# One stream tile for the residual's inputs, and the first mixer's adaLN units at one per product unit

## The chip, the cores and the metric

The kernel runs on one core of a Trainium2 chip. Its time is the device time of one execution in microseconds (us); where several runs were made, the median is given. A profile is one execution taken by the hardware profiler. The engines are named as there: PE (TensorE, matmuls), PEld (its weight loads), DVE (VectorE), ACT (ScalarE), POOL (GpSimd), SP (the engine that only issues transfers here).

## What is computed

A trunk of two layers on x of 256 tokens by 2048 columns, in float32. Each layer has two sub-layers, a token mixer and a SwiGLU feed-forward, and each sub-layer (numbered 0 to 3) is

```python
shift, scale, gate = split(silu(c) @ ada_w + ada_b)          # adaLN, from one row c
y = f(x * (1 + scale) + shift)
x = layer_norm(ALPHA * x + (1 + gate) * y, ln_g, ln_b)
```

Layer 0's mixer has an mLSTM group (8 heads) and an RWKV-7 group (16 heads) on one input projection, and one output projection; layer 1's has retention and gated DeltaNet heads. The feed-forward is `(silu(h @ wg) * (h @ wu)) @ wd` with 5632 hidden columns. All weights, some 650 MB, are read once.

## The kernel before

**Products.** All large products are made of *units*: a tile of 128 x 2048 weights (1 MB) is loaded into one of three `raw` tiles by SP (L690, in `raw`), split into a high and a low part, `hi` by ACT (L713) and `lo` by DVE (L714), and used by 24 matmuls of 128x128x512 (L728 to L730, in `part`). `product` (from L739) strings units together: four for 512 output columns of an input projection, two for half an output projection. It uses two of the three PSUM banks called `g`. After each unit it calls `fill(rate)`, which adds the rate to a credit and starts an adaLN unit for each whole credit, up to `ada_limit`.

**adaLN units.** `ada_unit` (from L635) computes 128 of the 6144 columns of one sub-layer's shift, scale and gate: a load of 1 MB and one multiply-and-sum on DVE over 128 x 2048 (L649). There are 192 units, 48 for each sub-layer. Units 0 to 31 run in the start-up (`first_products`). Where their tile is depends on `homes`: in the first mixer it is one of the same three `raw` tiles that the weights use, taken in program order; in the feed-forward parts it is `za` or `zt` in turn, two tiles of 8 KB per partition with one buffer each; in the second mixer it is `za` or `raw` in turn. The first mixer itself uses `za` for the channels of the RWKV heads (`chan`, L1394) and both mixers use `zt` for pairs of token blocks (`half`, L1134); the first product of a feed-forward part splits one weight tile into `zt`.

**First mixer.** `mixer_ab` (from L1801) runs four batches of RWKV heads. Between them (`after`) it makes eight products of four units, 32 units; it returns the last mLSTM group, `mlstm_group(1, direct)`, as a generator that makes four more products, 16 units, when `mix_out` advances it. With the rate 48.0 / 32 and the limit 80, the units 32 to 79 are all started within the first 32 product units. The gate of sub-layer 0 needs the units below 48, the norm at the end of `mix_out` all 80.

**Output and residual.** `mix_out` (from L1872) runs the output projection in two halves of the inner dimension, four blocks of 512 columns each. After each block of the first half, `first_sum` copies the banks to y (ACT) and `residual` (from L848) does, for each of the two 128-token tiles, y = y * gate (L858), adds ALPHA * (offset row) (L860), multiplies x by the scale row (L861) and adds ALPHA * x (L862). In sub-layer 0 there are no rows (x is the input itself) and only L858 and L862 are left. x comes by `x_block` (L827, 128 x 512) and the rows by `ln_rows` (L844, each broadcast to 128 x 512), each load 256 KB into a tile called `t2`, of which there are three, handed out in program order. After each block of the second half `last_sum` (from L864) multiplies the banks by the gate into a `t2` tile (L870), adds it to y (L871) and takes statistics (L872); L870 is what empties the bank. The feed-forward (`ffn`, from L951) runs its inner dimension in thirds and calls `residual` after the blocks of the second third. The gate row itself goes through DRAM (`gate_rows`, from L674).

**Order.** The program text is only a priority. `Plan` simulates all instructions with a cost for each, the tiles' buffers, and transfers at a fixed rate, and from that writes down for each engine, SP among them, a fixed order in which it then works (`impose`, L522). Tiles of one name are handed out in program order.

Of the kernel before, what the change touches and what calls it, by code (L numbers as in the profile page):

```python
# [16 lines left out]
ALU = mybir.AluOpType  # L17
# [4 lines left out]
P = 128  # L22
T = 256
NT = T // P
# [6 lines left out]
ALPHA = 4.0 ** 0.25  # L31
# [497 lines left out]
class Trunk:  # L529
# [292 lines left out]
        v.tensor_tensor(out, out, z[:], ALU.mult)  # L822


    def x_block(self, xsrc, t, n):
        xb = self.t2([P, 512])
        self.nc.sync.dma_start(xb[:], xsrc[P * t:P * t + P, 512 * n:512 * n + 512])  # L827
        return xb

    def first_sum(self, y, banks, n):  # L830
        for t in range(NT):
            self.nc.scalar.activation(y[t][:, 512 * n:512 * n + 512], banks[t][:], AF.Copy)
# [3 lines left out]
            o = y[t][:, 512 * n:512 * n + 512]  # L836
            self.nc.vector.tensor_tensor(o, banks[t][:], o, ALU.add)

    def ln_rows(self, sub, n):

        out = []
        for j in range(2):
            w = self.t2([P, 512])
            self.nc.sync.dma_start(w[:], self.ins["lnrow"][2 * sub + j:2 * sub + j + 1, 512 * n:512 * n + 512].to_broadcast([P, 512]))  # L844
            out.append(w)
        return out

    def residual(self, y, x, n):  # L848

        v = self.nc.vector  # L850
        xsrc, sub = x
        s = slice(512 * n, 512 * n + 512)
        if sub is not None:
            g, b = self.ln_rows(sub, n)
        for t in range(NT):
            xb = self.x_block(xsrc, t, n)
            o = y[t][:, s]
            v.tensor_tensor(o, o, self.gate[:, s], ALU.mult)  # L858
            if sub is not None:
                v.scalar_tensor_tensor(o, b[:], ALPHA, o, ALU.mult, ALU.add)  # L860
                v.tensor_tensor(xb[:], xb[:], g[:], ALU.mult)  # L861
            v.scalar_tensor_tensor(o, xb[:], ALPHA, o, ALU.mult, ALU.add)  # L862

    def last_sum(self, y, banks, n, stats, ts=range(NT)):  # L864
        v = self.nc.vector
# [1030 lines left out]
def body(tc, ins, out):  # L1896
    with ExitStack() as stack:
        k = Trunk(tc, ins, out, stack)
        k.setup()
        k.ada_limit = 32  # L1900
        h, early = k.first_products()
        x = (ins["x"], None)
        k.ada_limit = 80
        side = k.mixer_ab(h, 48.0 / 32, early)
        x, h = k.mix_out(ins["o_ab"], x, 0, side)
        x, h = k.ffn(0, x, h)
        k.ada_limit = 176
        k.mixer_cd(h, 32.0 / 44)
        x, h = k.mix_out(ins["o_cd"], x, 2)
        k.ffn(1, x, h)  # L1910
        plan = Plan(tc, tc.nc, 250, k.after)
        plan.prepare(0)
        order, _ = plan.run([x.bass_priority for x in plan.ins])
        plan.impose(order)
# [18 lines left out]
```

## Time and profile before

| | us |
|---|---|
| median of 3 runs | 2764.85 |
| lowest, highest | 2756.81, 2773.10 |
| the profiled execution | 2755.91 |
| its span | 2754.2 |
| DVE on adaLN units, the 82 in `raw` tiles | 187.4 |
| RWKV batches and their products | about 120 to 600 |
| output projection of layer 0, with the norm | about 600 to 735 |
| output projection of layer 1, with the norm | about 1895 to 2020 |

In what follows a row of a view by stretch gives the stretch, its length, and for PE, PEld, DVE, ACT and POOL the busy time and (x) the number of instructions, then the granted TensorE clock as a share of full speed, the mean busy share of the 16 DMA engines, and GB/s. A row of a view of waits gives the waiting engine, tile and line, what it waited for, and the time in total, the number of times and the longest. In a timeline a row gives the start, the duration, engine, line, operation, the tile written and those read, the count, and in brackets the idle time before it with what ended it. A row of the DMA issues gives the count, the size and the median time from issue to landing.

### The profile page before, as it was taken

How to read it: one execution, taken by the hardware profiler on the slowest of the kernel's cores; microseconds unless marked ns; L12 is line 12 of the kernel's file. 1: busy time of each engine (PE TensorE's matmuls, PEld its weight loads, DVE VectorE, ACT ScalarE, POOL GpSimd, SP SyncE). 2: the span in 40 equal slices, each digit the busy share in tenths (PEclk: the TensorE clock that was granted, in tenths of full speed). 3: DMA queues.
4: the chain of work that ended last, by engine and by line, in shares of the span. 5: the costliest groups of instructions: out<-in, count | busy, mean ns of one | idle time of the engine just before them, and what ended most of it. 6: DMA issues, size and time to landing. Idle time of an engine off the chain costs nothing.

```text
span 2754.2 us, 33686 instructions
## 1 busy us (share of the span) xinstructions
PE 2627.3 (95%) x12906; PEld 2155.3 (78%) x12906; DVE 2005.0 (73%) x3153; ACT 1272.4 (46%) x1706; POOL 76.8 (3%) x88
## 2 busy tenths in 40 slices
PE   5598999999999999999999999999999999999997
PEld 3476777788788888888888888888778888888886
DVE  7899887658777777767767989875866664557457
ACT  2364545557644444434446654444354444443442
POOL 0000100110000000000000101000000000000000
PEclk9899999999999999999999999999999999999999
DMA  9988775226578888778856776665657675556554
GB/s 394 358 297 300 253 287 207 92 93 211 202 302 303 311 320 315 286 251 309 311 194 227 272 282 220 259 231 204 226 200 274 259 271 188 196 213 240 192 186 165
DMA packets 109819, 681.60 MB, mean 247 GB/s; under 512 B 12437, under 2 KB 15705, under 8 KB 31577
## 3 DMA queue, kind: packets, MB, share of 16 engines
q1 hardware_dynamic: 108506, 677.36, 67.0%
q8 instruction: 101, 1.65, 0.2%
q10 hardware_dynamic: 1152, 2.10, 0.2%
q14 instruction: 60, 0.49, 0.0%
HBM read 668.89 MB, written 10.52 MB: 247 GB/s over the span
## 4 chain that ended last, share of the span: by engine, by line
PE 75%; DVE 6%; issue 3%; DMA 3%; ACT 2%; POOL 0%; DVEq 0%; SPq 0%; ACTq 0%; POOLq 0%
PE g L730 23%; PE g L728 23%; PE g L729 23%; DVE lo L714 1%; PE m L974 1%; ACT hi L713 1%; DMA t<-x 1%; DMA t<-lnrow 1%; DMA za<-ada 1%; DVE raw L649 0%; PE m L1254 0%; PE m L909 0%; PE c L1432 0%; DVE t L870 0%; DMA raw<-w_ab 0%
## 5 line engine op out<-in xcount | busy, mean ns | idle before, releaser
L714 DVE TENSOR_TENSOR lo<-raw,hi 128x1024 fp32r<-128x1024 f32 (+2 forms) x802 | 972.4, 1215 | 594.1 <-ACT hi L713 589.6
L713 ACT ACTIVATE hi<-raw 128x1024 fp32r<-128x1024 f32 (+2 forms) x802 | 842.3, 1053 | 1117.1 <-PE g L730 1028.5
L728 PE MATMUL g<-hi,h 128*128 128x512 f32 (+2 forms) x2312 | 908.8, 394 | 53.7 <-ACT h L792 39.5
L729 PE MATMUL g<-lo,h 128*128 128x512 f32 (+2 forms) x2312 | 907.0, 392 | 4.6 <-DVE lo L714 4.6
L730 PE MATMUL g<-hi,h 128*128 128x512 f32 (+2 forms) x2312 | 905.7, 392 | 0.0
L728 PEld LDWEIGHTS g<-hi,h 128*128 128x128 f32 x2312 | 439.3, 190 | 148.4 <-ACT h L792 42.4
L729 PEld LDWEIGHTS g<-lo,h 128*128 128x128 f32 x2312 | 440.2, 190 | 97.1 <-DVE lo L714 8.8
L730 PEld LDWEIGHTS g<-hi,h 128*128 128x128 f32 x2312 | 439.6, 190 | 86.6 <-issue 2.0
L728 PE MATMUL g<-hi,a 128*128 128x512 f32 x920 | 361.0, 392 | 5.8 <-DVE t L870 5.8
L729 PE MATMUL g<-lo,a 128*128 128x512 f32 x920 | 359.9, 391 | 0.5 <-DVE lo L714 0.5
L730 PE MATMUL g<-hi,a 128*128 128x512 f32 x920 | 359.8, 391 | 0.0
L728 PEld LDWEIGHTS g<-hi,a 128*128 128x128 f32 x920 | 173.4, 189 | 42.1 <-DVE t L870 6.3
L729 PEld LDWEIGHTS g<-lo,a 128*128 128x128 f32 x920 | 173.5, 189 | 36.2 <-DVE lo L714 0.9
L730 PEld LDWEIGHTS g<-hi,a 128*128 128x128 f32 x920 | 173.4, 188 | 35.8
L649 DVE SCALAR_TENSOR_TENSOR raw<-raw,silu_c 128x2048 f32<-128x2048 f32 x82 | 187.4, 2286 | 16.5 <-DMA raw<-ada 8.7
L649 DVE SCALAR_TENSOR_TENSOR za<-za,silu_c 128x2048 f32<-128x2048 f32 x56 | 127.9, 2284 | 3.5 <-DMA za<-ada 3.5
L649 DVE SCALAR_TENSOR_TENSOR zt<-zt,silu_c 128x2048 f32<-128x2048 f32 x38 | 86.8, 2284 | 1.4 <-DMA zt<-ada 1.4
L1438 DVE SCALAR_TENSOR_TENSOR f<-c,cols_sb,f 128x253 f32<-128x253 f32 (+2 forms) x120 | 56.1, 475 | 3.0 <-ACT f L1435 2.4
L1639 POOL TENSOR_SCALAR s<-cons_sb,log_alpha 128x128 f32<-128x128 f32 x16 | 15.9, 1006 | 1008.6 <-DVE log_alpha L1583 867.6
L649 DVE SCALAR_TENSOR_TENSOR a<-a,silu_c 128x2048 f32<-128x2048 f32 x16 | 36.4, 2286 | 0.2
L912 ACT ACTIVATE t<-m,affine 128x128 f32<-128x128 f32 x96 | 34.9, 470 | 0.1
L1254 PE MATMUL m<-y 64*128 64x256 f32 x128 | 30.6, 413 | 3.6 <-DVE a L1257 3.4
(480 smaller groups left out, 2095.7 us busy)
## 6 DMA issues: line engine op xcount, KB each, us to landing
raw<-gu SPq DMA_DIRECT2D x176, 1024.0 KB, 4.7
raw<-dn SPq DMA_DIRECT2D x88, 1024.0 KB, 4.8
raw<-ada SPq DMA_DIRECT2D x82, 1024.0 KB, 5.4
raw<-w_cd SPq DMA_DIRECT2D x60, 1024.0 KB, 4.8
za<-ada SPq DMA_DIRECT2D x56, 1024.0 KB, 7.0
raw<-w_ab SPq DMA_DIRECT2D x48, 1024.0 KB, 5.0
zt<-ada SPq DMA_DIRECT2D x38, 1024.0 KB, 6.9
a<-ada SPq DMA_DIRECT2D x16, 1024.0 KB, 17.0
```

The costliest lines, as they stand in the source:

```text
L649: v.scalar_tensor_tensor(w[:], w[:], 1.0, self.sc[:], ALU.mult, ALU.mult, accum_out=m[:, i:i + 1])
L713: nc.scalar.activation(hi[:, :2 * n], ws, AF.Copy)
L714: nc.vector.tensor_tensor(lo[:, :2 * n], ws, hi[:, :2 * n], ALU.subtract)
L728: mm(o, ah, wh, start=start and k == 0, stop=False)
L729: mm(o, ah, wl, start=False, stop=False)
L730: mm(o, al, wh, start=False, stop=stop and k == 3)
L912: nc.scalar.activation(h32[:, j, :], b[:, P * j:P * j + P], AF.Identity, bias=self.ab[:, sub + 1, 16 + k:17 + k], scale=self.ab[:, sub + 1 ...
L974: nc.tensor.transpose(b[:, P * k:P * k + P], gs[:, t, P * k:P * k + P], self.ident)
L1254: mm(b[:, T * x:T * x + T], bk[r, c, x, t, :], ar[r, c, t].rearrange("p x s -> p (x s)"), start=True, stop=True)
L1438: v.scalar_tensor_tensor(o[:, d:T], b[:, T * j:T * j + T - d], self.col(wname, 4 * (tile0 + i + j) + 3 - d), o[:, d:T], ALU.mult, ALU.add)
L1639: nc.gpsimd.tensor_scalar(L[:], sl, self.gl[:, t, 4 * g + j:4 * g + j + 1], None, ALU.mult)
```

## The change

`residual` no longer loads its blocks one by one. For every pair of blocks (n even) `stream` loads x for both token tiles and 1024 columns into one tile `za` (1 MB), and the two rows for 1024 columns into one tile `zt` (two loads of 512 KB); the arithmetic reads slices of these. And in the first mixer the rate of adaLN units goes from 48 / 32 to 48 / 48 for each product unit.

```diff
-    def x_block(self, xsrc, t, n):
-        xb = self.t2([P, 512])
-        self.nc.sync.dma_start(xb[:], xsrc[P * t:P * t + P, 512 * n:512 * n + 512])
-        return xb
...
-    def ln_rows(self, sub, n):
-
-        out = []
+    def stream(self, x, n):
+
+        xsrc, sub = x
+        s = slice(512 * n, 512 * n + 1024)
+        xs = self.own([P, NT, 1024], "za", 1)
+        self.nc.sync.dma_start(xs[:], xsrc[:, s].rearrange("(t p) c -> p t c", p=P))
+        if sub is None:
+            return xs, None
+        gb = self.own([P, 2, 1024], "zt", 1)
         for j in range(2):
-            w = self.t2([P, 512])
-            self.nc.sync.dma_start(w[:], self.ins["lnrow"][2 * sub + j:2 * sub + j + 1, 512 * n:512 * n + 512].to_broadcast([P, 512]))
-            out.append(w)
-        return out
+            self.nc.sync.dma_start(gb[:, j, :], self.ins["lnrow"][2 * sub + j:2 * sub + j + 1, s].to_broadcast([P, 1024]))
+        return xs, gb
 
     def residual(self, y, x, n):
 
         v = self.nc.vector
-        xsrc, sub = x
-        s = slice(512 * n, 512 * n + 512)
-        if sub is not None:
-            g, b = self.ln_rows(sub, n)
+        if n % 2 == 0:
+            self.rest = self.stream(x, n)
+        xs, gb = self.rest
+        s, c = slice(512 * n, 512 * n + 512), slice(512 * (n % 2), 512 * (n % 2) + 512)
         for t in range(NT):
-            xb = self.x_block(xsrc, t, n)
+            xb = xs[:, t, c]
             o = y[t][:, s]
             v.tensor_tensor(o, o, self.gate[:, s], ALU.mult)
-            if sub is not None:
-                v.scalar_tensor_tensor(o, b[:], ALPHA, o, ALU.mult, ALU.add)
-                v.tensor_tensor(xb[:], xb[:], g[:], ALU.mult)
-            v.scalar_tensor_tensor(o, xb[:], ALPHA, o, ALU.mult, ALU.add)
+            if gb is not None:
+                v.scalar_tensor_tensor(o, gb[:, 1, c], ALPHA, o, ALU.mult, ALU.add)
+                v.tensor_tensor(xb, xb, gb[:, 0, c], ALU.mult)
+            v.scalar_tensor_tensor(o, xb, ALPHA, o, ALU.mult, ALU.add)
...
-        side = k.mixer_ab(h, 48.0 / 32, early)
+        side = k.mixer_ab(h, 48.0 / 48, early)
```

## The prediction

> **What bounds the kernel now.** I read the page first, then what TensorE (PE) waited for, then PE and VectorE (DVE) by stretch around the two places that the edit touches.
>
> ```profile
> span 2754.2 us, 33686 instructions
> PE 2627.3 (95%) x12906; PEld 2155.3 (78%) x12906; DVE 2005.0 (73%) x3153; ACT 1272.4 (46%) x1706; POOL 76.8 (3%) x88
> ```
>
> PE is busy for 2627.3 of 2754.2 us, so all that any edit beside PE can win is the 127 us in which it idles, and time in which it runs at a lower granted clock. Who ends that idle time:
>
> ```profile
> PE g L728 <- ACT h L792: 50.0, 7, 14.4
> ...
> PE g L728 <- DVE t L870: 5.8, 1, 5.8
> ```
>
> The first line, 50 us, is the wait for the first activations at the start, which the edit leaves alone. The second is one single stall of 5.8 us behind `last_sum`; the edit of the residual touches it. Now the first mixer, by stretch. The columns of the first view are PE, PEld, DVE, ACT and POOL busy with their counts, then granted clock, DMA share and GB/s; the second view is the same for the adaLN line L649 alone, where each unit counts twice, its accumulator read being an instruction of its own.
>
> ```profile
> 120.00:205.00 85.00, 78.68 (x371) 61.70 (x372) 75.56 (x129) 50.15 (x89) 3.75 (x2) 0.96 0.84 298
> 205.00:260.00 55.00, 45.18 (x179) 33.81 (x177) 50.36 (x111) 20.46 (x25) 2.10 (x3) 0.94 0.81 301
> 260.00:300.00 40.00, 39.52 (x355) 33.29 (x355) 32.16 (x56) 19.71 (x38) 0.10 (x1) 1.00 0.75 272
> 300.00:371.00 71.00, 65.28 (x277) 48.31 (x274) 65.72 (x159) 32.04 (x56) 7.01 (x5) 0.98 0.78 284
> 371.00:470.00 99.00, 95.14 (x586) 74.64 (x585) 78.25 (x201) 50.57 (x94) 4.38 (x5) 0.97 0.66 232
> 470.00:547.00 77.00, 72.58 (x487) 57.48 (x486) 53.20 (x173) 44.64 (x90) 7.33 (x11) 0.93 0.27 91
> 547.00:650.00 103.00, 101.92 (x686) 86.45 (x685) 65.55 (x164) 64.75 (x110) 13.70 (x19) 1.00 0.37 129
> ```
> ```profile
> 205.00:260.00 55.00, 22.90 (x20) 0.94 0.81 301
> 260.00:300.00 40.00, 13.76 (x12) 1.00 0.75 272
> 300.00:371.00 71.00, 25.23 (x22) 0.98 0.78 284
> 371.00:470.00 99.00, 20.62 (x18) 0.97 0.66 232
> ```
>
> From 205 to 260 us DVE is busy 92% of the time, 22.9 of 50.4 us of it with ten adaLN units; PE idles 9.8 us. From 300 to 371 it is 93%, eleven units, 5.7 us idle. From 371 to 470 nine units remain and PE idles 3.9 of 99 us. After 470 there are none.
>
> ```profile
> PE g L728 <- ACT hi L713: 6.9, 3, 3.0
> ```
> ```profile
> ACT hi L713 <- DMA raw<-w_ab: 14.8, 4, 7.6
> ```
>
> These two lines are of the stretch 205 to 260: PE waits 6.9 us for weights, which ScalarE could not split because the load was late (14.8 us). A load is late there because weights and adaLN units take turns in three `raw` tiles, 1.5 units to one weight, and a tile comes free only when DVE has done its adaLN unit of 22.90 / 10 = 2.3 us.
>
> **The adaLN units spread out.** The same 48 units now go one to each of the mixer's 48 product units: 32 beside the eight products up to about 470, 16 beside the four of the last head group, which run until about 650. Nothing is added or removed; 16 x 2.3 = 37 us of DVE and 16 loads of 1 MB move from before 470 to after it.
>
> Gain. The stretch 371 to 470 already has about the new mixture. PE idles 3.9 / 99 = 3.9% there; 205 to 260 and 300 to 371 together idle 9.8 + 5.7 = 15.5 of 126 us, 12.3%. Brought to 3.9% they save 10.6 us; I take 9, as 260 to 300 and 120 to 205 (whose idle time is mostly the end of the start-up wait) give little, and 1 more for the granted clock of 0.94. Sum -10. Lower bound: PE's counts say that the units may already be hidden:
>
> ```profile
> 260.00:300.00 40.00, 7.79 (x19) 3.60 (x19) 1.00 0.75 272
> 300.00:371.00 71.00, 28.67 (x71) 13.47 (x71) 0.98 0.78 284
> 371.00:470.00 99.00, 31.05 (x76) 14.79 (x76) 0.97 0.66 232
> ```
>
> That is L728, eight of which make a product unit. The stretch from 260 to 371, one batch of heads, holds 90 / 8 = 11.25 units in 111 us, the next batch 9.5 in 99. A unit is 24 matmuls and takes a full PE 5.44 us (weight loads further below are issued 5.44 us apart), so beside the products the batches took 111 - 61.2 = 49.8 and 99 - 51.7 = 47.3 us; seventeen adaLN units against nine made 2.5 us, 0.3 us each. By that 16 units less are worth 5 us. Upper bound: all the idle time and lost clock from 120 to 371, without the 5.5 us that is the end of the start-up, 16 + 8 = 24 us. I stay near the first, whose rows are the nearest.
>
> ```profile
> PE g L728 <- ACT h L792: 5.5, 1, 5.5
> ```
>
> Cost. From 470 to 650 DVE is idle 23.8 + 37.5 = 61 us, room for 37. But some of that is while PE works through the heads' chain and takes no weights, and then the three `raw` tiles let few units through. PE idles 4.4 + 1.1 us there now. At 3.9% of 180 us it would idle 7.0, +1.5; I take +3, bounds 0 and 30 (thirteen units at their full 2.3, were only three done in the gaps). SP has the same number of issues, later; adaLN loads now stand between the direct products' weight loads, and a weight load waits for the unit two tiles ahead of it. What needs the last units is the norm at about 717, some 70 us behind them: free; without that cover the norm would wait 2.3 us for each.
>
> ```profile
> 717.68 2.11 ACT y L904 x3
> ```
>
> **The residual's stream.** Before, each 512-column block loads x (two tiles) and, with scale and offset rows, two more, through the three `t2` tiles that `last_sum` needs as well. 56 loads of 256 KB become 8 of 1 MB and 12 of 512 KB; 36 issues on SP fall away beside other work. DVE's arithmetic is the same. Where it held PE up:
>
> ```profile
> 1962.48 0.39 PE L730 MATMUL g<-hi,a 128*128 128x512 f32 x1
> 1968.69 0.79 PE L728 MATMUL g<-hi,a 128*128 128x512 f32 x1 [5.82 <-DVE t L870]
> 1969.29 0.63 PE L729 MATMUL g<-lo,a 128*128 128x512 f32 x1
> 1969.71 0.63 PE L730 MATMUL g<-hi,a 128*128 128x512 f32 x1
> ...
> 1974.68 0.39 PE L730 MATMUL g<-hi,a 128*128 128x512 f32 x1
> ```
> ```profile
> 1927.63 1.29 DVE L858 TENSOR_TENSOR y<-y,a 128x512 f32<-128x512 f32 x2
> ...
> 1965.29 1.29 DVE L860 SCALAR_TENSOR_TENSOR y<-t,y 128x512 f32<-128x512 f32 x2 [3.90 <-DMA t<-lnrow]
> ...
> 1967.95 0.69 DVE L870 TENSOR_TENSOR t<-g,a 128x512 f32<-128x512 f32 x1
> ```
>
> This is layer 1's mixer output. PE's last matmul starts at 1962.48 and the next at 1968.69, because the bank is emptied by L870, whose `t2` tile stands in line behind the last block's rows (3.90 us of DMA wait). Then fourteen matmuls until 1974.68 take 6.0 us, 0.43 us each; at the usual 5.44 / 24 = 0.227 (below) they take 3.2: 2.8 us lost. With the stream out of `t2`, L870 of block 0 can start when its product ends: 5.8 + 2.8 = 8.6 us. What is late next: the gate row lands at about 1927 (first L858), and blocks 0 and 1 then need 16 instructions of 0.65, 10 us, by some 1942. Then two loads follow each other in the same tiles.
>
> ```profile
> t<-x SPq DMA_DIRECT2D x32, 256.0 KB, 4.9
> raw<-o_cd SPq DMA_DIRECT2D x16, 1024.0 KB, 5.5
> ```
>
> 1 MB lands in 5.5 us, hardly more than 256 KB; x and rows together in 6 to 10, so by 1952, and the 10 us of work at the half of DVE that weights leave is done by about 1972. Block 2's last sum, two products of 10.9 us after 1962, needs it at about 1984: 12 us to spare. On SP the second x load waits for block 1's last instruction, and weight loads, one per 5.44 us, are queued behind it; three `raw` tiles cover a few us of that.
>
> ```profile
> 1935.90 0.33 SPq L690 DMA_DIRECT2D raw<-o_cd  x1
> ...
> 1941.34 0.33 SPq L690 DMA_DIRECT2D raw<-o_cd  x1
> ```
>
> Layer 0's feed-forward part (third 1, around 1250) loses one PE wait:
>
> ```profile
> PE g L729 <- DVE lo L714: 1.5, 1, 1.5
> ```
>
> 1.5 us. The other two residual places show PE no wait of this kind: nothing to win. In feed-forward, adaLN tiles `za` and `zt` are now locked until block 3 is done; fifteen units wait for that with 24 product units (130 us) ahead of them: free, or 2.3 us each if they were late. Sum 8.6 + 1.5 = 10.1 us: -10, bounds -10 and 0.
>
> **Sum.** -10 + 3 - 10 = -17 us. The profiled execution took 2755.9 us (span 2754.2), 8.9 under the median of the runs shown, 2764.85; on the median I forecast 2748.
>
> **Rivals.**
> *Larger gain.* If more than the idle time comes back. PE's weight loads (PEld) are busy 61%, 68% and 73% of 205-260, 300-371 and 120-205, against 75% of 371-470; raised to 75% these stretches shorten by 10 + 7 + 3 = 20 us. With +3 and -10: -27, 2738. The Trainium skill (Trainium Kernel Development and Optimization, Best Practices) tells one to judge by weight-load busy time and not by matmul busy time; here the two differ, 20 us against 9, and the sum by that rule would be 2738. Against it: the heads' small matmuls change the mixture of PEld from stretch to stretch.
>
> *The units were hidden.* The batch comparison holds: 0.3 us for each unit, saved early and paid late, which cancels. Only the residual part is left, -10, 2755.
>
> *The stall comes back as a wait for the second stream.* Two tiles, one buffer each: the load of blocks 2 and 3 can't start before block 1 is done, and DVE, in order, waits for all of it, 6 to 10 us, with the weights' splits (L714) behind it; PE then loses some 8 us in layer 1's output. Total -17 + 8 = -9, 2756. Best Practices of the same page of the Trainium skill asks for double buffers so that loads lie beside compute, which speaks against this edit. Against the rival: the planner knows the load and puts other work ahead, and block 2 has 12 us to spare.
>
> *Slower: late units in front of the chain.* From 470 to 650 the chain of heads and the last group's convolutions run on DVE; thirteen units of 2.3 us that stand before a step of theirs cost 30 us, while the early ones, hidden, give back 5. With -10 that is +15, 2780. It decides from 15 / 16 = 0.9 us per moved unit upward. For it: DVE runs over 90% wherever PE took weights. Against: 371 to 470 bears nine units with 3.9 us of idle time.
>
> **How the numbers follow.** Forecast 0.45; larger gain 0.15; units hidden 0.16; second stream 0.13; slower 0.11. A measurement of this kernel can tell about 0.5%, 13.8 us, from no change: faster is below 2751, slower above 2779. The forecast's own range, -25 to -9 (2740 to 2756), lies three quarters below that: faster 0.34 + 0.15 = 0.49. Slower is most of the last rival, 0.09. Same is the rest, 0.42. The range reaches from all gains at their upper bound with no cost (-24 - 10 = -34, 2731) to the near part of the slower rival, 2771.
>
> **What the changed profile would show.** Right: adaLN units spread evenly to about 640; 205 to 371 shorter by some 9 us with the wait for `hi` nearly gone; no wait for L870 in layer 1's output and no half-clock matmuls there; PE idle below 7 us from the 470 mark to the start of the output projection. Wrong: PE waits on L713 or L714 after 470, a DVE wait of over 5 us for the second stream, or an early stretch as long as before.

## The result, and the profile after

| | runs | median us | ratio to the kernel before, 95% interval |
|---|---|---|---|
| before (the three runs of the first table and one more) | 4 | 2768.01 | |
| the change | 4 | 2725.97 | 0.9872 (0.9823 to 0.992) |
| the change, timed again (e0) | 4 | 2723.63 | 0.9852 (0.9827 to 0.9876) |

The kernel became faster by 1.3 to 1.5%, 35 to 41 us, by the two ratios, where 17 were forecast; the median lies 5 us under the low end of the range. The profiled execution of the change took 2744.2 us, the slowest of its four; its page begins

```profile
span 2742.5 us, 33594 instructions
PE 2631.8 (96%) x12906; PEld 2164.2 (79%) x12906; DVE 2002.3 (73%) x3153; ACT 1272.7 (46%) x1706; POOL 72.3 (3%) x88
```

and PE's waits on weights and activations, first before, then after, are

```profile
PE g L728 <- ACT hi L713: 10.3, 6, 3.0
```
```profile
PE g L728 <- ACT h L792: 46.7, 7, 13.0
...
PE g L728 <- ACT hi L713: 1.3, 2, 0.8
```

The wait of these matmuls for the high part of their weights has gone from 10.3 to 1.3 us, and there is no line for `last_sum` any more. Lines from `residual` on have moved up by one: L857 is the former L858, L869 the former L870.

**Layer 1's output.** From the first residual instruction to the norm, first before, then after:

```profile
1927.60:2000.30 72.70, 66.33 (x279) 53.65 (x277) 62.00 (x91) 30.06 (x32) 0.00 (x0) 0.93 0.66 230
```
```profile
1924.50:1989.00 64.50, 62.95 (x278) 51.74 (x277) 59.47 (x88) 30.08 (x32) 0.00 (x0) 1.00 0.66 238
```

The same matmuls, 278 or 279 by the counts, take 64.5 us in place of 72.7, at a granted clock of 1.00 in place of 0.93. DVE's timeline after shows why:

```profile
1924.48 1.29 DVE L857 TENSOR_TENSOR y<-y,a 128x512 f32<-128x512 f32 x2
...
1942.69 1.29 DVE L859 SCALAR_TENSOR_TENSOR y<-zt,y 128x512 f32<-128x512 f32 x2 [1.80 <-DMA zt<-lnrow]
...
1954.47 0.68 DVE L869 TENSOR_TENSOR t<-g,a 128x512 f32<-128x512 f32 x1
```

L869 comes 30.0 us after the gate row, before it was 40.3 us (1927.63 to 1967.95). The wait for the second stream, of which one rival made 8 us for PE, is 1.8 us of DVE and none of PE.

**The first mixer.** Here I show e0, the same kernel with a profiled execution near its median (2722.7 us span). The stretches end where PE makes the first transposes of the inverse of a batch of heads (L1028, after the change L1027), to within 3 us, so a row holds the same heads in both kernels. Before, the rows not shown yet:

```profile
120.00:260.00 140.00, 123.87 (x548) 95.51 (x548) 125.92 (x239) 70.61 (x113) 5.85 (x5) 0.95 0.83 300
260.00:371.00 111.00, 104.80 (x628) 81.60 (x629) 97.88 (x214) 51.75 (x94) 7.11 (x6) 0.98 0.77 280
...
547.00:717.60 170.60, 169.52 (x999) 142.78 (x997) 126.96 (x281) 100.03 (x153) 14.63 (x20) 1.00 0.47 166
```

The change (e0), all engines and then the adaLN line alone (two instructions for each unit):

```profile
120.00:237.00 117.00, 109.95 (x523) 88.03 (x524) 103.67 (x219) 67.30 (x110) 5.13 (x5) 0.99 0.74 269
237.00:336.40 99.40, 98.42 (x616) 78.85 (x615) 82.47 (x195) 51.75 (x92) 3.78 (x6) 1.00 0.67 243
336.40:432.00 95.60, 92.70 (x593) 73.94 (x592) 80.01 (x197) 51.42 (x95) 5.42 (x5) 1.00 0.68 248
432.00:511.70 79.70, 74.99 (x503) 59.49 (x502) 64.61 (x186) 44.95 (x89) 7.43 (x11) 0.96 0.51 183
511.70:690.50 178.80, 175.46 (x1012) 147.45 (x1010) 148.85 (x312) 100.40 (x154) 12.73 (x20) 0.98 0.57 207
```
```profile
120.00:237.00 117.00, 34.44 (x30) 0.99 0.74 269
237.00:336.40 99.40, 25.22 (x22) 1.00 0.67 243
336.40:432.00 95.60, 22.92 (x20) 1.00 0.68 248
432.00:511.70 79.70, 11.67 (x11) 0.96 0.51 183
511.70:690.50 178.80, 20.43 (x18) 0.98 0.57 207
```

The units are spread as the edit says: 15, 11, 10 and then some 15 in the last two rows (before, 25, 17, 9 and none). The first three stretches end at 432 in place of 470, 38 us earlier; the last two take 258.5 in place of 247.6 us, so 11 are given back and the norm begins 27 us earlier. In the first profile of the same kernel the third stretch ends at 450, 20 us earlier than before: its granted clock there is 0.94 and 0.92 in the second and third stretch, where e0 has 1.00. So what a row shows in time depends on the execution.

**Two parts of a time.** TensorE's granted clock in these records is either full or half, and for each execution the mean is listed. The time multiplied by this mean is an estimate of the time that the execution would take at full clock, if everything scaled with it; the difference is put down to half clock. In the chain of heads it does scale: a pair of matmuls of 128x64 (L1283) starts every 0.22 us in e0 at full clock and every 0.43 us in e11 at half. Idle time that falls into half clock does not, and the estimate counts only half of it. Among the runs of one kernel the first number has a standard deviation of 2 to 5 us, the second one of 3 to 12, so I use both; differences of the first are given with two standard errors:

| kernel | median us | ratio (95%) | full-clock us, mean | lost at half clock, mean |
|---|---|---|---|---|
| before (13 runs, beside e0 to e3) | 2763.1 | | 2705.4 | 58.7 |
| e1 residual alone | 2751.9 | 0.9952 (0.9934 to 0.997) | 2701.2 | 49.9 |
| e2 rate alone | 2738.9 | 0.9905 (0.9882 to 0.9928) | 2686.7 | 51.6 |
| e0 both | 2723.6 | 0.9852 (0.9827 to 0.9876) | 2680.7 | 42.9 |
| e3 both, rate 48/40 | 2747.3 | 0.9942 (0.9921 to 0.9963) | 2687.9 | 61.3 |
| e4 rate 48/32, short sums | 2743.5 | 0.9914 (0.9886 to 0.9942) | 2693.3 | 50.3 |
| e5 rate 48/32, short loads | 2747.5 | 0.9944 (0.9916 to 0.9971) | 2685.5 | 64.0 |
| e8 rate 48/32, both short | 2730.9 | 0.9886 (0.9859 to 0.9914) | 2675.6 | 57.9 |
| e6 both, no late units | 2725.3 | 0.9845 (0.9812 to 0.9878) | 2675.4 | 49.0 |
| e7 both, small stream loads | 2728.8 | 0.9859 (0.9826 to 0.9892) | 2681.2 | 47.1 |
| e10 both, rate 48/56 | 2743.5 | 0.9942 (0.992 to 0.9964) | 2692.0 | 56.0 |
| e11 both, short loads | 2762.9 | 0.9993 (0.9975 to 1.0011) | 2681.5 | 81.5 |
| e9 rate 48/32, loads elsewhere | 2880.9 | 1.0425 (1.0401 to 1.0449) | 2760.7 | 121.6 |

The rows come from three chips: e0 to e3 from one, e4 to e7 from a second, e8 to e11 from a third, each ratio against the kernel before on the same chip. At full clock the kernel before takes 2705.4, 2705.4 and 2704.9 us on the three, so that column can be read across them.

### The profile page after: what moved, and what is told of

Same layout as the page of the kernel before. It is cut to its first block, busy times and chain, and to the rows that moved or that the text cites. A ratio compares the mean times of both kernels' runs of the same rounds, so it can differ in the third digit from the quotient of the medians.

```text
span 2742.5 us, 33594 instructions
## 1 busy us (share of the span) xinstructions
PE 2631.8 (96%) x12906; PEld 2164.2 (79%) x12906; DVE 2002.3 (73%) x3153; ACT 1272.7 (46%) x1706; POOL 72.3 (3%) x88
## 4 chain that ended last, share of the span: by engine, by line
PE 78%; DVE 10%; DMA 8%; ACT 2%; issue 2%; SPq 0%; POOL 0%; DVEq 0%; ACTq 0%
PE g L728 24%; PE g L729 23%; PE g L730 23%; DVE lo L714 2%; DMA raw<-ada 2%; DMA a<-ada 2%; DVE raw L649 2%; DMA raw<-w_ab 1%; ACT hi L713 1%; DMA za<-ada 1%; PE m L973 1%; DMA y<-w_ab 1%; PE m L1253 0%; PE m L1086 0%; PE m L1271 0%
## 5 line engine op out<-in xcount | busy, mean ns | idle before, releaser
L714 DVE TENSOR_TENSOR lo<-raw,hi 128x1024 fp32r<-128x1024 f32 (+2 forms) x802 | 971.5, 1214 | 580.6 <-ACT hi L713 577.1
L713 ACT ACTIVATE hi<-raw 128x1024 fp32r<-128x1024 f32 (+2 forms) x802 | 842.6, 1052 | 1111.4 <-PE g L730 1035.5
L728 PE MATMUL g<-hi,h 128*128 128x512 f32 (+2 forms) x2312 | 911.0, 394 | 41.2 <-ACT h L792 37.3
L728 PEld LDWEIGHTS g<-hi,h 128*128 128x128 f32 x2312 | 440.6, 191 | 132.8 <-ACT h L792 40.1
L728 PE MATMUL g<-hi,a 128*128 128x512 f32 x920 | 359.3, 391 | 0.0
L649 DVE SCALAR_TENSOR_TENSOR raw<-raw,silu_c 128x2048 f32<-128x2048 f32 x82 | 187.4, 2286 | 32.1 <-DMA raw<-ada 24.3
L728 PEld LDWEIGHTS g<-hi,a 128*128 128x128 f32 x920 | 172.7, 188 | 35.5
L649 DVE SCALAR_TENSOR_TENSOR za<-za,silu_c 128x2048 f32<-128x2048 f32 x56 | 127.9, 2284 | 4.5 <-DMA za<-ada 4.5
L649 DVE SCALAR_TENSOR_TENSOR zt<-zt,silu_c 128x2048 f32<-128x2048 f32 x38 | 86.8, 2285 | 2.6 <-DMA zt<-ada 2.4
L649 DVE SCALAR_TENSOR_TENSOR a<-a,silu_c 128x2048 f32<-128x2048 f32 x16 | 36.3, 2285 | 0.0
L1094 POOL TENSOR_SCALAR_AFFINE_SELECT a<-a 128x512 f32<-128x512 f32 (+1 forms) x20 | 22.4, 1127 | 332.4 <-ACT a L1255 300.0
```

What stands on the lines that cost most here:

```text
L649: v.scalar_tensor_tensor(w[:], w[:], 1.0, self.sc[:], ALU.mult, ALU.mult, accum_out=m[:, i:i + 1])
L713: nc.scalar.activation(hi[:, :2 * n], ws, AF.Copy)
L714: nc.vector.tensor_tensor(lo[:, :2 * n], ws, hi[:, :2 * n], ALU.subtract)
L728: mm(o, ah, wh, start=start and k == 0, stop=False)
L1094: self.nc.gpsimd.affine_select(x, x, pattern=[[0, n] for n in dims] + [[1, P]], compare_op=ALU.is_gt if strict else ALU.is_ge, fill=0.0, b ...
```

## The experiments

**Which part is worth what.** Four kernels on one chip.

> The changed kernel once more, so that its parts are timed beside it on one chip. Both theories: ratio to the kernel before 0.983 to 0.992, as in its first runs.

> The residual's stream alone, adaLN rate left at 48/32. Theory (the rate is worth most): only layer 1's stall goes, -8 to -12 us, ratio 0.995 to 0.997; heads of the first mixer stand where they stood (fourth batch's inverse near 545 us). Rival (the residual is worth most): -25 us or more, ratio 0.991 or below.

> The adaLN rate 48/48 alone, residual as before. Theory: ratio 0.988 to 0.993 (-20 to -33 us), with the wait for L870 in layer 1's output still there. Rival: ratio 0.996 to 0.998 (-5 to -10 us).

```diff
-        side = k.mixer_ab(h, 48.0 / 48, early)      # e1, in the changed kernel
+        side = k.mixer_ab(h, 48.0 / 32, early)
...
-        side = k.mixer_ab(h, 48.0 / 32, early)      # e2, in the kernel before
+        side = k.mixer_ab(h, 48.0 / 48, early)
```

The residual alone gives 0.9952, 13 us; the rate alone 0.9905, 26 us; their product, 0.9857, is what both together measure (0.9852). The rate is worth most, as the theory had it, and within these intervals the parts don't touch each other. In e2 the output of layer 1 still has its stall:

```profile
PE g L728 <- DVE t L870: 5.7, 1, 5.7
```
```profile
1913.70:1985.90 72.20, 66.17 (x278) 53.55 (x277) 62.41 (x91) 30.18 (x32) 0.00 (x0) 0.95 0.67 231
```

In e1 the same stretch takes 65.1 us, at a granted clock of 1.00.

> The changed kernel with a rate between the two, 48/40: 8 instead of 16 units beside the last group's products. If the relief of the early mixer is worth more than the late units cost, per unit and without a best point between, the ratio lies half way between e1 and e0 (about 0.991). If late units cost as much as early ones save beyond some number, it is at or below e0's (0.987).

```diff
-        side = k.mixer_ab(h, 48.0 / 48, early)
+        side = k.mixer_ab(h, 48.0 / 40, early)
```

Neither side is met: 0.9942 is no better than the residual alone within the intervals. By the full-clock column 13 ± 3 of the 20 us between e1 and e0 are there, so most of the relief is; but 61.3 us are lost at half clock where e0 loses 42.9. In its profile, in the third batch:

```profile
360.00:370.00 10.00, 8.12 (x119) 6.38 (x120) 6.13 (x13) 4.37 (x10) 0.00 (x0) 0.50 0.54 176
370.00:380.00 10.00, 10.00 (x56) 8.81 (x54) 2.23 (x9) 4.15 (x9) 0.00 (x0) 0.50 0.24 95
380.00:390.00 10.00, 10.00 (x45) 9.38 (x45) 1.16 (x3) 4.13 (x8) 0.00 (x0) 0.54 0.01 2
```

PE is busy and the clock (third column from the right) is half. This spell lasts from 358 to 389 us; PE had idled for 1.6 us shortly before it and idles for 2.8 us just after it begins, waiting for DVE in the inverse of the heads.

**Why an early unit costs more than I counted.** All on e1, rate 48/32; what is cut belongs to the first mixer's 48 units alone.

> e1 (rate 48/32) with the multiply-and-sum of the first mixer's 48 units cut from 2048 to 256 columns; their loads of 1 MB and their raw tiles stay, and the planner still counts the full length (it leaves out seven eighths of these sums). Theory DVE (the units cost because DVE's 2.3 us each are missing to the chain and the splits): the early batches shorten by 25 us or more, ratio to before 0.986 or below. Rival raw tiles (the units cost because their loads hold a tile of the weights' ring): less than 10 us better than e1, ratio 0.992 to 0.995.

```diff
-        v.scalar_tensor_tensor(w[:], w[:], 1.0, self.sc[:], ALU.mult, ALU.mult, accum_out=m[:, i:i + 1])
+        k = slice(0, 256) if 32 <= u < 80 else slice(0, D)
+        v.scalar_tensor_tensor(w[:, k], w[:, k], 1.0, self.sc[:, k], ALU.mult, ALU.mult, accum_out=m[:, i:i + 1])
```

> e1 with the loads of these 48 units cut from 1 MB to 64 KB, the sum at its full length on a resident row (it leaves out the weights of these units). Theory DVE: hardly better than e1, ratio 0.992 to 0.995. Rival raw tiles: a tile is free some 3 us sooner and 48 MB less are moved; 20 us or more better, ratio 0.988 or below.

```diff
-            w = self.raw(src)
+            w = self.raw(src[:, 0:128] if 32 <= u < 80 else src)
...
+        v.scalar_tensor_tensor(w[:], self.sc[:] if 32 <= u < 80 else w[:], 1.0, self.sc[:], ALU.mult, ALU.mult, accum_out=m[:, i:i + 1])
```

> e1 (rate 48/32) with both the loads of the 48 units (64 KB) and their sums (128 columns) cut; their raw tiles are still taken in turn, and the planner counts the sums in full (it leaves out nearly all of these units' work). Compared by time multiplied by mean granted clock, in which e1 is 2701, e4 2693, e5 2686 and the changed kernel 2681. Theory (a unit costs by how long it keeps a tile of the weights' ring: load, wait for DVE, sum): the two cuts add up to about -24, 2677 or below. Rival (what is left is the order that the planner makes for 1.5 units per product unit): no better than e5, 2684 to 2690.

e8 is e5's load with the sum over 128 columns. By time e4 gives some 8 us beyond e1, e5 nothing that the intervals show, and neither of the two theories as written held. By full-clock time the sums are worth 8 us, the loads 16, and both together 26 (each ± 3): they add up, as the theory of the tile's hold said (2677 or below; measured 2675.6). One thing besides changes with the loads: the planner saw them shorter and made another order, in which the first batch's inverse begins at 282 us in e5 and 273 in e8, against 261 in e1. The 16 us are for load and order together. What ACT waited for `w_ab` loads from 120 to 480 us goes the same way; e1, e5 and e8 in this order (in e8 the added line moves L713 to L714):

```profile
ACT hi L713 <- DMA raw<-w_ab: 34.8, 11, 8.1
```
```profile
ACT hi L713 <- DMA raw<-w_ab: 23.7, 10, 5.0
```
```profile
ACT hi L714 <- DMA raw<-w_ab: 6.3, 3, 3.5
```

(e4, whose loads are whole, has 49.2.) So DVE's 2.3 us, which the prediction gave as what keeps a tile, is the smaller part of what a unit costs here; the load, which lands 5.1 us after its issue in e1 from 130 to 430 us and 2.0 us in e5, is the larger.

> e5 (short loads into the raw tiles, rate 48/32) and beside each a copy of the unit's 1 MB of weights to a scratch place in DRAM, which takes no tile (the sums still use a resident row). Theory tile: as e5, 2684 to 2688 by time multiplied by granted clock. Rival traffic (the units cost because 1.5 MB per product unit more are moved): back to e1, 2698 or above.

```diff
+        if 32 <= u < 80:
+            far = self.dram.tile([P, D], F32, name=self.name("far"))
+            nc.sync.dma_start(far[:], src)
```

This one tells nothing: the copies wait for no tile, so the order put them all at the start, where PE was busy for 11 of the 140 us from 60 to 200 and the DMA engines were full. So this run does not part the tile from the traffic. The traces of e1 and e5 speak for the tile: from 130 to 430 us the DMA engines are busy for 0.75 of the time in e1 and 0.36 in e5, and yet a weight load (`raw<-w_ab`) lands 5.1 and 5.0 us after its issue, at the median. It is not slower for the traffic; it is issued late. In e1 SP waits 66.2 us in that stretch, 18 times, for an adaLN sum (L649) to free a `raw` tile; in e0 51.5 us, 10 times.

> The changed kernel (rate 48/48) with the 48 units' loads cut to 64 KB (it leaves out their weights). Theory tile: at two tiles per product unit the ring no longer holds the products up, so at most 4 us less than e0's 2681 by time multiplied by granted clock. Rival (a shorter load helps whatever the rate): 10 us or more less, 2671 or below.

The same cut of the loads as e5, in the changed kernel. Full-clock time 2681.5 against e0's 2680.7: at one unit per product unit a shorter load brings nothing more (0.8 us worse, ± 2), as the theory of the tile's hold said. That is the other half of the answer, though for another order of the products too: with two tiles per product unit the ring holds the products up by no more than these 2 us. By time the kernel is 39 us slower than e0, and by this measure all of it is half clock. Some stretches of its profile, all engines, and two of L728, the product matmuls, alone:

```profile
385.00:395.00 10.00, 10.00 (x43) 9.50 (x43) 3.63 (x9) 2.65 (x6) 0.00 (x0) 0.50 0.02 7
...
485.00:495.00 10.00, 9.41 (x49) 7.87 (x47) 1.38 (x5) 6.33 (x12) 0.00 (x0) 0.50 0.00 0
495.00:505.00 10.00, 9.92 (x48) 9.87 (x47) 2.40 (x8) 1.58 (x5) 0.00 (x0) 0.50 0.01 2
...
466.00:514.00 48.00, 45.16 (x294) 40.59 (x294) 14.44 (x46) 12.76 (x28) 0.00 (x0) 0.50 0.09 26
```
```profile
385.00:395.00 10.00, 0.77 (x1) 0.33 (x1) 0.50 0.02 7
...
485.00:495.00 10.00, 0.00 (x0) 0.00 (x0) 0.50 0.00 0
...
475.00:525.00 50.00, 0.00 (x0) 0.00 (x0) 0.53 0.06 22
```

With the loads short, the order has used up products earlier: 319 matmuls of L728 stand ahead of the third batch's inverse, in e0 297, and 38 in the 96 us after it, in e0 52 in 80. The heads' chain then runs with few products or none beside it, PE counts as busy, and it stays at half clock.

**What the late units cost.**

> The changed kernel without the 16 adaLN units that stand beside the last group's products (it leaves out units 64 to 79, load and sum). If they cost what the marks of the batches say (the lead of the third batch shrinks by 12 us up to the norm): ratio 0.980 to 0.982 beside e0's 0.985. If they are hidden: 0.984 to 0.986.

```diff
+        if not 64 <= u < 80:
+            if deep and i % 2:
...
+            v.scalar_tensor_tensor(w[:], w[:], 1.0, self.sc[:], ALU.mult, ALU.mult, accum_out=m[:, i:i + 1])
```

Hidden, by time: 0.9845 beside 0.9852. By full-clock time they cost 5.3 ± 4.6 us, less than the 12 that I had read off the marks. The marks also hold product units that moved from early to late stretches: 11 matmuls of L728, 1.4 units or 7.5 us, and 11 less 7.5 leaves 3.4 us.

> The changed kernel with the units spread further: 48/56, eight of the 56 product units being those of the output projection's first half (nothing left out). If still fewer units per product unit help: 5 us or more below e0, ratio 0.983 or below. If 48/48 has already freed the ring, 0.984 to 0.988; if the output projection can't bear them, above 0.988.

```diff
-        side = k.mixer_ab(h, 48.0 / 48, early)
+        side = k.mixer_ab(h, 48.0 / 56, early)
...
-                banks = self.product([w[u], w[u + 1]], 512, acts, 0.0, tail=...)
+                banks = self.product([w[u], w[u + 1]], 512, acts, 48.0 / 56 if sub == 0 and half == 0 else 0.0, tail=...)
```

Worse, 0.9942 and 11 ± 3 us more at full clock: the third case of the expectation. In its profile PE has these waits in the last 65 us before the norm, 650 to 715, most of it the output projection. Below them stand these 65 us as a whole, and then the last 65 us before the norm in e0:

```profile
PE g L729 <- DVE lo L714: 3.4, 2, 2.9
PE g L728 <- ACT hi L713: 2.8, 2, 1.4
```
```profile
650.00:715.00 65.00, 57.45 (x236) 44.42 (x234) 57.27 (x119) 27.91 (x33) 0.00 (x0) 0.92 0.59 210
```
```profile
625.00:690.00 65.00, 65.00 (x293) 53.81 (x292) 57.70 (x103) 32.79 (x38) 0.00 (x0) 1.00 0.63 225
```

PE idles 7.6 us, 6.2 of them for weights that DVE and ACT have not yet split; in e0 it idles not at all. DVE is as busy in e0 (57.7 us), so its busy time alone does not tell a stretch that bears the units from one that doesn't. The forecast's bound of 30 us was for the stretch ahead of the output projection; this run shows such a cost in the output projection itself. Where the rest of the 11 us lies I did not separate.

**What the residual's part is.**

> The changed kernel with the same two stream tiles filled by loads of 256 KB as before the change (eight per pair of blocks in place of three). Theory (the gain is that the stream is out of t2): as e0, ratio 0.983 to 0.987. Rival (the gain is the larger load): back to the rate alone, 0.989 to 0.992.

```diff
-        self.nc.sync.dma_start(xs[:], xsrc[:, s].rearrange("(t p) c -> p t c", p=P))
+        for c in range(2):
+            for t in range(NT):
+                self.nc.sync.dma_start(xs[:, t, 512 * c:512 * c + 512], xsrc[P * t:P * t + P, 512 * (n + c):512 * (n + c) + 512])
```

(and the same for the rows). 0.9859 and 2681.2: the same as e0. The larger loads have no part in it within ± 4 us; with them ruled out, what is left is that the stream has left `t2`, whose wait (L870) is in both kernels without the stream tiles and in none with them. The stretch from the gate row to the norm in layer 1's output takes 63.6 to 65.1 us in each of the twelve profiles with the stream tiles, and 72.2 and 72.7 in the two without.

## Where the prediction was right, and where wrong

**The early relief was mis-sized.** "Sum -10" was the term that failed. On e0's rows the stretches up to the third batch shorten by 38 us. The 1.4 product units that moved behind them are 7.5 us of this, which leaves 30. Of these 15 are PE's idle time, 26.2 to 10.9 us, and 11 are half clock (0.95, 0.98 and 0.97 of the rows before, 0.99, 1.00 and 1.00 after), the two overlapping by a us or two; some 4 I can't assign. The half clock is not the change's alone: the first profile of the same kernel has idle time nearly as low, 14.0 us, but granted clocks of 0.98, 0.94 and 0.92, and its stretches shorten by 20 us, 12 without the moved units. At full clock the two profiles agree: some 20 and 18 us without the moved units. My sum took 9 of idle time, by bringing the busy stretches down to the third one's 3.9%, and 1 for the clock. It was half of what came: the third stretch before still had nine units in 9.5 product units and waits of its own, so its 3.9% was no floor. e0 idles 1.0% in the second batch, and nearly all of the 15.5 us came back that the two busy stretches idled. My upper bound, 24, is passed by e0's time and holds at full clock.

The rival called *larger gain* had the direction: weight-load busy time read 20 us for this relief, and its 75% is about what came (75%, 79% and 77% in e0's three rows). The Trainium skill's advice to judge the distance to the roofline by weight-load busy time and not by matmul busy time (Trainium Kernel Development and Optimization, Best Practices) was the better reading here: 20 us against my 9, where the two profiles show some 20 and 18 at full clock. In part that is luck, as its total, 2738 with the late cost and the residual, still lies 12 us above the median.

**The lower bound's argument fell.** Two batches with seventeen and nine units differed by 2.5 us after their products were taken off, from which I had 0.3 us for each unit. The changed kernel's second batch has eleven units and takes 99.4 us with 88 L728, 39.5 beside its products, against 49.8 before: ten us for six units. The comparison had used a batch that was itself held up, by half clock for one thing (0.97).

**The cause was named half.** I had the ring of three `raw` tiles in the text, with DVE's 2.3 us as the price. e4, e5 and e8 show 8 us for the sums and 16 for the loads, these with the order that came with them, by full-clock time. That it is the tile and not the traffic is read from the landing times of the weight loads; no run parts the two.

**The late cost was right.** +3 with bounds 0 and 30: 5.3 ± 4.6 by e6 at full clock, none by medians. PE idles 8.0 us in the last two stretches of e0 where I allowed 7, and none of it for weights. *Slower* and *units hidden* are ruled out, the first by e6, the second by e2.

**The residual was right in its place.** -10 was forecast, e1 gives 13 (8 to 18). The stall in layer 1's output was put at 8.6 us; it is 8.2 in the first profile and 7.6 in e1's. By full-clock time e1 gains only 4.2 ± 2.7, and 8.8 are half clock. The two belong together: the stretch's 72.7 us at a clock of 0.93 are 67.6 at full clock against 65.1, so by this measure 2.5 of its 7.6 us are work and 5.1 half clock, in which the prediction saw 2.8. The way between layer 0's two norms is 1.7 us shorter (735.1 for 736.8), where 1.5 were forecast. From there to the gate row of layer 1 the twelve profiles with streams take 471 to 484 us and the two without 473 and 475, so there neither gain nor cost can be told. *A wait for the second stream* did not come: 1.8 us of DVE, none of PE. The Trainium skill asks for double buffers, so that loads overlap compute (the same page and section). The trace shows no price for leaving them out here: block 2's residual was done by 1949.3 us and its last sum took it at 1979.2, 30 us later where the forecast had 12 to spare, so one buffer was enough.

**The baseline.** I made the sum against an execution that lost 49.6 us at half clock, while the kernel before loses 58.7 on the mean and the changed one 42.9 to 49.2. Between 10 and 16 us of the measured gain are this, for which the sum had only the 1 us of the first mixer and the 2.8 us behind the stall. That the new order leaves fewer stretches of chain alone is my reading of it, from e3 and e11, not shown for e0 by an experiment of its own; and since the first profile has the same order and yet two spells of half clock in the early batches, the order alone does not decide it.

## What to carry to other kernels

A background unit that shares a small ring of tiles with the main stream should be priced by how long it keeps a tile, load and waits included, and not by its engine time alone. Here, with 1.5 units to one weight in three tiles, spreading them was worth 20 us at full clock; at one to one nothing was left to win by shorter loads. If a step on the critical engine takes its scratch tile in line behind transfers that it doesn't need, give those a tile of their own; the size of the loads did not matter here. Before a forecast is made against one profile, multiply each run's time by its granted clock: e0 and e11 differ by 1 us at full clock and by 39 us in time.

## What the hardware showed that I had not expected

Half clock can last through a serial chain while PE is busy by the profile. In e11 the records show it from 374 to 401 us, PE busy throughout and few product matmuls beside the chain, and from 466 to 514, of which PE is busy for 45 of 48 us; from 475 to 525 there is not one L728. The two spells do not begin alike. Ahead of the second PE idles 5.8 us, from 462.4 to 468.2; in the 10 us ahead of the first it idles 0.6 us. The Trainium skill (TensorE: Matmul & The Clock Gate, Part 1) has the clock go to half after an idle window of some 3.4 us and back to full after one busy window. The stall of 5.8 us in the kernel before with the six us of half clock behind it agrees with that, and so does the start of the second spell. The start of the first and the length of both do not, if busy is what the profile counts. What share of use the gate asks for, no run here tells.
